# Layer 1 of a two-layer encoder: TensorE's order written out, with own buffers for the gate weights

## The chip, the cores and the metric

The kernel runs on one core of one Trainium2 chip. The metric is the device time of one execution in microseconds (us). TensorE (PE) does the matmuls, ScalarE (ACT) activations, copies and casts, VectorE (DVE) elementwise work and scans, GpSimd (POOL) some elementwise work and small copies; SyncE (SP) only issues the DMAs. Each engine has its own instruction stream; semaphores join them.

## The reference

Two mixing layers over 2048 tokens of width 1024, each closed by a residual and a layer norm. The change concerns layer 1 (the odd layer), cut here to what matters:

```python
u = h @ od_w_in                      # h: modulated x, 2048 x 1024; u: 2048 x 2048
xC, gC = split(u, 2)
xc = causal_conv4(xC, conv_w) + conv_b          # per channel, over time
gate_r = sigmoid(blockdiag(xc, wa) + ba)        # 4 blocks of 256 x 256
gate_i = sigmoid(blockdiag(xc, wx) + bx)
log_a  = -8 * gate_r * softplus(-lam)
a      = exp(log_a)
v      = sqrt(-expm1(2 * log_a)) * (gate_i * xc)
hC     = scan(h_t = a_t * h_(t-1) + v_t)
y      = (hC * silu(gC)) @ od_w_out
x      = layer_norm(alpha * x + (1 + gate) * y)
```

## The kernel before

Channels lie on the 128 partitions, tokens along the free axis. The tokens are worked in two halves of 1024, "blocks of a layer" here, each of two sub-blocks b of 512. The order is layer 0 first half, layer 0 second half, layer 1 first half, layer 1 second half; after each comes an output stage (the product with the output weights in tiles po, the residual r, the layer norm with lg and lb), during which the next half's x is loaded, transposed on TensorE (xp) and scaled to h. Layer 0 is the same before and after.

Every product is done to nearly full fp32 precision by splitting both operands into a rounded part and a residue (names with h and l: hh_h and hl_h for the input, wh_ and wl_ for weights, xh_c and xl_c for the convolved input) and running three matmuls (`mm3`: rounded × residue, rounded × rounded, residue × rounded). A weight piece of 128 × 512 is loaded to a `raw` tile (two buffers for the whole program), cast to wh on ACT, and its residue wl is made on POOL; wh and wl tiles have four buffers each.

In a block of layer 1 `mix1` runs four groups g. A group has two projections (pp_c, channel tiles ct = 2g and 2g+1; 48 matmuls each, 24 for each b). Each 24 are copied from PSUM into u_c on ACT, with a three-token carry (cr_c) on POOL. Then `mix_c` takes the group: it loads the gate weights (raw_wg, wh_wg, wl_wg), convolves u_c into xc_c (one ACT instruction and three on DVE for each channel tile and b), splits xc_c, does the gate matmuls pg_c (two gates × two channel tiles × two inputs × three for each b, 48 for both) with a sigmoid on ACT behind each bank of two PSUM banks, and then over 128 × 2048 elements tanh, exp and square on ACT, two multiplies and an add on DVE, sqrt on ACT (which needs another activation table), the multiply that makes the scan's input (L1191; called gth in the prediction), and two scans on DVE.

After the four groups come eight gate projections (pp_g with silu, `gate_steps`), whose product with the stored scan is the input of the output stage.

The program is written in this order, and a scheduler reorders each engine's instructions by priority; in layer 1 of before TensorE's order is the scheduler's too, while layer 0 writes TensorE's order out by hand. The weight loads run ahead by a priority of 100.

Of the kernel before, what the change touches and what calls it, by code (L numbers as in the profile page):

```python
# [68 lines left out]
def tile_encoder(  # L69
# [19 lines left out]
    nc = tc.nc  # L89
# [10 lines left out]
    wp = ctx.enter_context(tc.tile_pool(name="wp", bufs=4))  # L100
# [16 lines left out]
    tp = _Cur()  # L117
    ps = ctx.enter_context(tc.tile_pool(name="ps", bufs=1, space=PSUM))
# [249 lines left out]
    def split(hi, lo, src, eng=None, hi_eng=None):  # L368
        (hi_eng or nc.scalar.copy)(hi, src)  # L369
        return (eng or nc.vector).tensor_tensor(out=lo, in0=src, in1=hi.bitcast(F32), op=ALU.subtract)  # L370
# [38 lines left out]
                mixer_constants()  # L409
        return hi, lo  # L410

    def load_w(src, name, nk=KT, raws=None, ahead=0):
        with tc.high_priority(offset=ahead):
            return split_w(src, name, nk, raws)

    def split_w(src, name, nk, raws):
        wh, wl = [], []
        for i in range(2):
            n = min(4, nk - 4 * i)
            if raws is None:  # L420
                raw = wp.tile([P, 4, P], F32, name=f"raw_{name}_{i}", tag="raw", bufs=2)[:, 0:n]
                nc.sync.dma_start(raw, src[:, 4 * i : 4 * i + n])
            else:
                raw = raws[:, 4 * i : 4 * i + n]
            hi = wp.tile([P, 4, P], F32R, name=f"wh_{name}_{i}", tag="wh")
            lo = wp.tile([P, 4, P], F32R, name=f"wl_{name}_{i}", tag="wl")
# [24 lines left out]

    def proj(*a, **k):
        for _ in proj_steps(*a, **k):
            pass
# [173 lines left out]
    for i in range(1):  # L628
        t = cst.tile([P, BLK], F32, name=f"st_{i}")
# [170 lines left out]
    for i in range(2):  # L800
        t = cst.tile([P, 8, 64], F32, name=f"tt_{i}")
# [342 lines left out]

    c_state = [None] * 8

    def mix_c(g, sb, us):
        wh, wl = load_w(w_gate[g], f"wg{sb}_{g}", ahead=100)
        nm = f"c{g}_{sb}"
        xc = tp.tile([P, 2, SBT], F32, name=f"xc_{nm}", tag="c_x")  # L1150
        gr = tp.tile([P, 2, SBT], F32, name=f"gr_{nm}", tag="c_gr")
        gi = tp.tile([P, 2, SBT], F32, name=f"gi_{nm}", tag="c_gi")
        for b in range(2):
            ls = slice(b * BLK, (b + 1) * BLK)
            xh = []
            xl = []
            for i in range(2):
                ct = 2 * g + i
                u = us[i][b]
                x_ = xc[:, i, ls]  # L1160
                nc.scalar.activation(
                    x_, u[:, 3 : BLK + 3], AF.Identity, scale=V("conv_w", 24 + ct), bias=V("conv_b", ct)
                )
                for w in range(3):
                    nc.vector.scalar_tensor_tensor(  # L1165
                        out=x_, in0=u[:, w : w + BLK], scalar=V("conv_w", 8 * w + ct), in1=x_,
                        op0=ALU.mult, op1=ALU.add,
                    )
                hi = tp.tile([P, BLK], F32R, name=f"xh{i}_{nm}_{b}", tag=f"c_h{i}", bufs=2)
                lo = tp.tile([P, BLK], F32R, name=f"xl{i}_{nm}_{b}", tag=f"c_l{i}", bufs=2)  # L1170
                split(hi, lo, x_)
                xh.append(hi)
                xl.append(lo)
            for i in range(2):
                ct = 2 * g + i
                for gt, t in enumerate((gr, gi)):
                    pt = ps.tile([P, BLK], F32, name=f"pg_{nm}_{b}_{i}_{gt}", tag="tb", bufs=2)
                    for k in range(2):
                        wi = gt * 4 + k * 2 + i
                        mm3(pt, wh[wi], wl[wi], xh[k], xl[k], k == 0, k == 1)  # L1180
                    nc.scalar.activation(t[:, i, ls], pt, AF.Sigmoid, bias=V(("ba", "bx")[gt], ct))
# [25 lines left out]
    def evac_u(key, ct, nshift, dst):  # L1207
        def evac(b, pt):
            u = up.tile([P, BLK + 3], F32, name=f"u_{key}_{b}", tag="u")
            nc.scalar.copy(u[:, nshift : nshift + BLK], pt)  # L1210
            if nshift:
                prev = carry.get(ct)
                if prev is None:
                    nc.gpsimd.memset(u[:, 0:nshift], 0.0)
                else:
                    nc.gpsimd.tensor_copy(u[:, 0:nshift], prev)
                cr = sp_.tile([P, nshift], F32, name=f"cr_{key}_{b}", tag=f"cr{nshift}_{ct[1]}", bufs=2)
                nc.gpsimd.tensor_copy(cr, u[:, BLK : BLK + nshift])
# [87 lines left out]
        return tail, plan  # L1306

    def mix1(sb, hs, w_first):
        for g in range(4):
            us = [[None, None] for _ in range(2)]  # L1310
            for i in range(2):
                ct = 2 * g + i
                proj(
                    w_od[ct], f"c{sb}_{ct}", hs, evac_u(f"c{sb}_{ct}", (1, ct), 3, us[i]),
                    w_first[0] if ct == 0 else None, ahead=100,
                )
            mix_c(g, sb, us)
        tail = []
        plan = out_weights(1, sb, w_odo, lambda: [
            tp.tile([P, 4, BLK], F32, name=f"wo1_{sb}_{tag}", tag=tag) for tag in ("c_x", "c_gr", "c_gi", "c_th")  # L1320
        ])
        for _ in gate_steps(1, sb, hs, w_od, lambda k: 8 + k, range(KT), tail, plan):
            pass
        return tail, plan

    pre, pre_phase = None, const_phase
# [1 line left out]
    for i, (l, sb) in enumerate(order):  # L1328
        if l:
            w_first = [load_w(w_od[0], f"c{sb}_0")]  # L1330
        elif sb:
            w_first = [load_w(wf_dr[1], f"z{sb}_1")]
        else:
            w_first = [load_w(None, f"z0_{i}", raws=wf[:, i]) for i in (1, 0)]
        hs = make_h(l, sb, pre)
# [4 lines left out]
        with phase(f"mix{l}_{sb}"):  # L1340
            tail, wo = (mix0, mix1)[l](sb, hs, w_first)
# [80 lines left out]
```

## Time and profile before

| | |
|---|---|
| median of 3 runs | 2350.18 us (2343.73 to 2357.08) |
| profiled execution, its own time | 2348.29 us |
| its span in the trace | 2346.6 us |
| busy share | PE 93%, DVE 63%, ACT 54%, POOL 24% |
| mean granted TensorE clock | 0.969 of full speed |
| layer 1, first block | 1672.5 to 1857.1 us, PE busy 169.07 of 184.60 |
| layer 1, second block | 2007.05 to 2194.15 us, PE busy 170.61 of 187.10 |

Times are taken from the start of the span. A row of a timeline gives start, length, engine, line, operation, its output and input tiles (numbers of buffers left out), and in brackets the idle time ahead of it on its engine with what ended it. The numbers behind a stretch are, in this order, its length, the busy time of PE, PEld (weight load), DVE, ACT and POOL, each with its count of instructions, the granted clock, the DMA engines' share and GB/s. A busy matmul reads 0.39 us but the next starts 0.23 us behind it, since they overlap.

### The profile page before, as it was taken

The page shows a single profiled execution, that of the slowest core. Times are in us where ns is not written, and L with a number is a line of the kernel's source. Part 1 is how long each engine was busy: PE and PEld are TensorE (multiplying, and loading weights), DVE is VectorE, ACT ScalarE, POOL GpSimd, SP SyncE. Part 2 cuts the span into 40 slices and gives each one's busy share as a digit, 9 for nine tenths or more (in the row PEclk, how much of TensorE's full clock was granted, in tenths as well). Part 3 has the DMA queues.
Part 4 walks back from the last instruction along what each step waited for, and adds up shares of the span by engine and source line. Part 5 has one row for each costly group of instructions (what it writes and reads, how often), then busy time and mean ns, then how long its engine had stood idle before and what let it go on. Part 6 is the DMA issues. An engine that isn't in the chain of part 4 may idle for free. (4 is left out here: it accounts for less than half of the span.)

```text
span 2346.6 us, 45509 instructions
## 1 busy us (share of the span) xinstructions
PE 2172.6 (93%) x18400; PEld 1727.5 (74%) x18400; DVE 1485.6 (63%) x2750; ACT 1271.8 (54%) x2033; POOL 564.5 (24%) x586
## 2 busy tenths in 40 slices
PE   5989999999999999799999998899999999989998
PEld 4767777777777877577777777678777788767786
DVE  6646676677643678477676666436756556766366
ACT  4344656456666634355665456674467643666541
POOL 3311122212111332112212111112334331353321
PEclk7999999999999999899999999999999999999999
DMA  8310111111332637111111114326312564112652
GB/s 299 95 38 28 35 41 35 43 32 37 110 107 86 221 117 251 35 30 37 35 41 40 40 30 116 112 96 227 133 58 70 173 209 157 63 59 95 206 179 99
DMA packets 185938, 229.82 MB, mean 98 GB/s; under 512 B 65912, under 2 KB 99320, under 8 KB 185728
## 3 DMA queue, kind: packets, MB, share of 16 engines
q1 hardware_dynamic: 185728, 226.92, 30.0%
q8 instruction: 144, 2.36, 0.4%
q14 instruction: 66, 0.54, 0.1%
HBM read 175.46 MB, written 51.39 MB: 97 GB/s over the span
## 5 line engine op out<-in xcount | busy, mean ns | idle before, releaser
L433 PE MATMUL pp_g<-hl_h,wh_g 128*128 128x512 f32 x512 | 210.5, 411 | 4.0 <-ACT go L597 4.0
L435 PE MATMUL pp_g<-hh_h,wl_g 128*128 128x512 f32 x512 | 203.3, 397 | 4.0 <-POOL wl_g L370 4.0
L434 PE MATMUL pp_g<-hh_h,wh_g 128*128 128x512 f32 x512 | 203.0, 397 | 0.0
L370 POOL TENSOR_TENSOR wl_g<-raw_g,wh_g 128x512 fp32r<-128x512 f32 x64 | 97.3, 1525 | 343.9 <-ACT wh_g L369 294.7
L433 PE MATMUL po<-hl_wo,wh_mx 128*128 128x512 f32 x448 | 175.9, 393 | 2.6 <-DVE y L529 2.6
L435 PE MATMUL po<-hh_wo,wl_mx 128*128 128x512 f32 x448 | 175.3, 391 | 0.0
L434 PE MATMUL po<-hh_wo,wh_mx 128*128 128x512 f32 x448 | 174.8, 390 | 0.0
L433 PE MATMUL pp_b<-hl_h,wh_b 128*128 128x512 f32 x384 | 162.6, 423 | 6.2 <-ACT cr_b L851 6.2
L433 PE MATMUL pp_a<-hl_h,wh_a 128*128 128x512 f32 x384 | 165.2, 430 | 0.3 <-ACT cr_b L851 0.3
L435 PE MATMUL pp_a<-hh_h,wl_a 128*128 128x512 f32 x384 | 153.8, 401 | 0.0
L434 PE MATMUL pp_a<-hh_h,wh_a 128*128 128x512 f32 x384 | 153.5, 400 | 0.0
L435 PE MATMUL pp_b<-hh_h,wl_b 128*128 128x512 f32 x384 | 151.8, 395 | 0.0
L434 PE MATMUL pp_b<-hh_h,wh_b 128*128 128x512 f32 x384 | 151.7, 395 | 0.0
L370 POOL TENSOR_TENSOR wl_mx<-raw_mx,wh_mx 128x512 fp32r<-128x512 f32 x64 | 82.2, 1290 | 254.5 <-ACT wh_mx L369 254.5
L370 POOL TENSOR_TENSOR wl_b<-raw_b,wh_b 128x512 fp32r<-128x512 f32 x48 | 69.5, 1451 | 248.6 <-ACT wh_b L369 214.1
L370 POOL TENSOR_TENSOR wl_a<-raw_a,wh_a 128x512 fp32r<-128x512 f32 x48 | 65.9, 1375 | 238.9 <-ACT wh_a L369 238.1
L433 PEld LDWEIGHTS pp_g<-hl_h,wh_g 128*128 128x128 f32 x512 | 98.6, 193 | 27.5 <-ACT go L597 4.8
L435 PEld LDWEIGHTS pp_g<-hh_h,wl_g 128*128 128x128 f32 x512 | 98.1, 192 | 27.3 <-POOL wl_g L370 5.7
L589 DVE TENSOR_TENSOR go<-go,oi 128x512 f32<-128x512 f32 x64 | 46.9, 733 | 110.1 <-DMA oi<-o_dr 65.8
L434 PEld LDWEIGHTS pp_g<-hh_h,wh_g 128*128 128x128 f32 x512 | 98.4, 192 | 18.8
L435 PE MATMUL pp_c<-hh_h,wl_c 128*128 128x512 f32 x256 | 100.8, 395 | 10.9 <-POOL wl_c L370 9.6
L433 PE MATMUL pp_c<-hl_h,wh_c 128*128 128x512 f32 x256 | 101.4, 396 | 2.8 <-DVE hl_h L370 2.6
(368 smaller groups left out, 5731.7 us busy)
## 6 DMA issues: line engine op xcount, KB each, us to landing
adw<-in_ada_w_dram SPq DMA_DIRECT2D x96, 256.0 KB
oi<-o_dr SPq DMA_DIRECT2D x64, 256.0 KB
m_dr<-go SPq DMA_DIRECT2D x56, 256.0 KB
raw_b<-in_w_ev_dram SPq DMA_DIRECT2D x48, 256.0 KB
raw_a<-in_w_ev_dram SPq DMA_DIRECT2D x48, 256.0 KB
raw_g<-in_w_ev_dram SPq DMA_DIRECT2D x32, 256.0 KB
wo<-in_w_evo_dram SPq DMA_DIRECT2D x32, 256.0 KB
raw_mx<-m_dr SPq DMA_DIRECT2D x32, 256.0 KB
```

The costliest lines, as they stand in the source:

```text
L370: return (eng or nc.vector).tensor_tensor(out=lo, in0=src, in1=hi.bitcast(F32), op=ALU.subtract)
L433: nc.tensor.matmul(pt, ah, bl, start=first, stop=False)
L434: nc.tensor.matmul(pt, ah, bh, start=False, stop=False)
L435: nc.tensor.matmul(pt, al, bh, start=False, stop=last)
L589: nc.vector.tensor_mul(go[b], go[b], oi[b])
```

## The change

`mix_c` is split into `c_inputs` (tiles and gate weights) and a generator `c_steps` for each group and b, and `mix1` writes out TensorE's order: a table of steps lets the gate matmuls of a b, in two portions of 12, follow 12 matmuls of a projection each. The first projection of the next group is now under way before a group's first gates, and the last group's gates lie inside the first gate projection. The weights of a projection are loaded one projection ahead. The gate weights' wh and wl get tiles of their own (tags c_wh and c_wl, four buffers each), so that the four of wp are left to the projections; the raw tiles stay shared. The convolved input xc_c has two buffers.

```diff
-    def split_w(src, name, nk, raws):
+    def split_w(src, name, nk, raws, own):
...
-            hi = wp.tile([P, 4, P], F32R, name=f"wh_{name}_{i}", tag="wh")
-            lo = wp.tile([P, 4, P], F32R, name=f"wl_{name}_{i}", tag="wl")
+            hi, lo = (
+                tp.tile([P, 4, P], F32R, name=f"w{c}_{name}_{i}", tag=f"c_w{c}", bufs=4)
+                if own else wp.tile([P, 4, P], F32R, name=f"w{c}_{name}_{i}", tag=f"w{c}")
+                for c in "hl"
+            )
...
+    def c_inputs(g, sb):
+
         nm = f"c{g}_{sb}"
-        xc = tp.tile([P, 2, SBT], F32, name=f"xc_{nm}", tag="c_x")
+        wg = load_w(w_gate[g], f"wg{sb}_{g}", ahead=100, own=True)
+        xc = tp.tile([P, 2, SBT], F32, name=f"xc_{nm}", tag="c_x", bufs=2)
...
+    def c_steps(g, sb, b, us, group):
...
+            xh.append(hi)
+            xl.append(lo)
+            yield (8, 6)[i]
...
+                nc.scalar.activation(t[:, i, ls], pt, AF.Sigmoid, bias=V(("ba", "bx")[gt], ct))
+            if i == 0:
+                yield 2
+        if b == 0:
+            return
         nc.vector.tensor_mul(gi, gi, xc)
...
+            for ct in range(8):
+                g, i = divmod(ct, 2)
+                if i == 0:
+                    groups[g] = c_inputs(g, sb)
+                later = load_w(w_od[ct + 1], f"c{sb}_{ct + 1}", ahead=100) if ct < 7 else None
+                key = f"c{sb}_{ct}"
+                yield from proj_steps(None, key, hs, evac_u(key, (1, ct), 3, us[g][i]), w)
+                w = later
+            yield from gate_steps(1, sb, hs, w_od, lambda k: 8 + k, range(KT), tail, plan)
+
+        tasks = [[16 * g + 4 * b + 4, (g, b)] for g in range(4) for b in range(2)]
...
+        with tc.manual_schedule(engines={nc.tensor.engine}):
```

On TensorE a block read before: projections ct 0 and 1, 12 gate matmuls, 5 of ct 2, the other 36 gate matmuls, and the next gates 103 matmuls on. It now reads: ct 0 to 1, then ct 2 with 12 gate matmuls behind each 12 of its own (12 + 12 + 12 + 12 for the 48 of the group), ct 3 whole (24 + 24), 12 of ct 4, and the next group's first 12 gates. The engines that serve it moved along; two places on ACT and one on SP follow. In the names, wh_c_1_0 is piece 0 of the weights of ct 1, wh_wg_0_1 piece 1 of the gate weights of group 0, u_c_1_0 sub-block 0 of ct 1; of xc_c, xh_c, xl_c, gr_c and gi_c the group's number is left out.

ACT at the start of layer 1's first block, before: the casts of wh_c_1 stand among those of the input ahead of the first copy of a projection.

```order
L369 CAST wh_c_1_0_18051<-raw_c_1_0_18049 128x512
L369 CAST hh_h_0_1_4_17933<-h_0_1_4_17798 128x512
L369 CAST wh_c_1_1_18057<-raw_c_1_1_18055 128x512
...
L1210 COPY u_c_0_0_18014<-pp_c_0_0_17989 128x512
L369 CAST wh_wg_0_0_18123<-raw_wg_0_0_18121 128x512
L1161 ACTIVATE xc_c_0_18133<-u_c_0_0_18014,vec 128x512
L369 CAST wh_wg_0_1_18129<-raw_wg_0_1_18127 128x512
L1210 COPY u_c_0_1_18044<-pp_c_0_1_18019 128x512
```

The same place in the changed kernel.

```order
L1223 COPY u_c_0_0_18043<-pp_c_0_0_18018 128x512
L1223 COPY u_c_0_1_18081<-pp_c_0_1_18056 128x512
L369 CAST wh_wg_0_0_17993<-raw_wg_0_0_17991 128x512
L369 CAST wh_wg_0_1_17999<-raw_wg_0_1_17997 128x512
L1169 ACTIVATE xc_c_0_18003<-u_c_0_0_18043,vec 128x512
L1169 ACTIVATE xc_c_0_18003<-u_c_0_1_18081,vec 128x512
L369 CAST wh_c_1_0_18008<-raw_c_1_0_18006 128x512
L369 CAST wh_c_1_1_18014<-raw_c_1_1_18012 128x512
```

The casts of wh_c_1 moved behind both copies of ct 0, both casts of the gate weights and both first steps of the convolution.

SP at the same time, before: the DMAs that bring the raw pieces, among stores of the residual (x_dr) and loads for the output stage.

```order
L422 DMA raw_c_1_0_18049<-in_w_od_dram 128x512
L422 DMA raw_c_1_1_18055<-in_w_od_dram 128x512
L554 DMA x_dr<-r_1_6_17716 128x1024
L422 DMA raw_wg_0_0_18121<-in_w_gate_dram 128x512
L422 DMA raw_wg_0_1_18127<-in_w_gate_dram 128x512
L554 DMA x_dr<-r_1_7_17812 128x1024
L422 DMA raw_c_2_0_18252<-in_w_od_dram 128x512
L513 DMA r_0_0_19786<-x_dr 128x1024
```

And in the changed kernel.

```order
L422 DMA raw_wg_0_0_17991<-in_w_gate_dram 128x512
L422 DMA raw_wg_0_1_17997<-in_w_gate_dram 128x512
L557 DMA x_dr<-r_1_6_17716 128x1024
L557 DMA x_dr<-r_1_7_17812 128x1024
L422 DMA raw_c_1_0_18006<-in_w_od_dram 128x512
L422 DMA raw_c_1_1_18012<-in_w_od_dram 128x512
L422 DMA raw_c_2_0_18094<-in_w_od_dram 128x512
```

The gate weights moved ahead of ct 1. The loads r_0_0, r_0_1, lg_0 and lb_0 for the output stage, which stood here, moved to right ahead of x_1_0_0, the first load of x for the next half, in the output stage itself.

ACT behind the last gate matmul of group 0, before: from the last sigmoid to the sqrt.

```order
L1181 ACTIVATE gi_c_0_18135<-pg_c_0_1_1_1_18224,vec 128x512
L1186 ACTIVATE th_c_0_18235<-gr_c_0_18134 128x2048
L1187 ACT_TABLE_LOAD
L1187 ACTIVATE gr_c_0_18134<-gr_c_0_18134 128x2048
L1210 COPY u_c_2_0_18289<-pp_c_2_0_18264 128x512
L1188 ACTIVATE xc_c_0_18133<-gr_c_0_18134 128x2048
L369 CAST wh_wg_1_0_18398<-raw_wg_1_0_18396 128x512
L369 CAST wh_wg_1_1_18404<-raw_wg_1_1_18402 128x512
L1210 COPY u_c_2_1_18319<-pp_c_2_1_18294 128x512
L1190 ACT_TABLE_LOAD
L1190 ACTIVATE th_c_0_18235<-th_c_0_18235 128x2048
```

And in the changed kernel, a row further, to the next group's xh_c.

```order
L1190 ACTIVATE gi_c_0_18005<-pg_c_0_1_1_1_18333,vec 128x512
L369 CAST wh_wg_2_1_18465<-raw_wg_2_1_18463 128x512
L1199 ACTIVATE th_c_0_18344<-gr_c_0_18004 128x2048
...
L369 CAST xh_c_0_1_18365<-xc_c_0_18194 128x512
L1201 ACTIVATE xc_c_0_18003<-gr_c_0_18004 128x2048
L369 CAST wh_c_5_0_18474<-raw_c_5_0_18472 128x512
L1223 COPY u_c_3_0_18406<-pp_c_3_0_18381 128x512
L1169 ACTIVATE xc_c_0_18194<-u_c_3_0_18406,vec 128x512
L369 CAST wh_c_5_1_18480<-raw_c_5_1_18478 128x512
L1203 ACT_TABLE_LOAD
L1203 ACTIVATE th_c_0_18344<-th_c_0_18344 128x2048
L369 CAST xh_c_0_0_18415<-xc_c_0_18194 128x512
```

A cast of gate weights moved between sigmoid and tanh; two casts of ct 5, an xh_c and an xc_c of the next group moved into the chain; the second xh_c of the next group's sub-block 0 stands behind the sqrt.

## Rows read from the trace of the kernel before

**Rows 1.** The page's first part: busy us, share of the span, instructions.

```profile
PE 2172.6 (93%) x18400; PEld 1727.5 (74%) x18400; DVE 1485.6 (63%) x2750; ACT 1271.8 (54%) x2033; POOL 564.5 (24%) x586
```

**Rows 2.** The table of stretches: layer 1's first block, an output stage, its second block.

```profile
1672.50:1857.10 184.60, 169.07 (x724) 133.86 (x722) 120.75 (x118) 124.93 (x156) 72.58 (x67) 1.00 0.28 92
...
1911.40:2006.00 94.60, 93.89 (x441) 77.80 (x440) 65.47 (x100) 40.98 (x64) 25.27 (x21) 1.00 0.46 160
2007.05:2194.15 187.10, 170.61 (x723) 134.88 (x721) 121.20 (x118) 124.73 (x156) 75.48 (x67) 0.99 0.23 77
```

**Rows 3.** TensorE's waits, 1672.5 to 2194.15: us in total, times, longest.

```profile
PE pg_c L433 <- DVE xl_c L370: 9.8, 8, 1.6
PE pp_c L435 <- POOL wl_c L370: 9.6, 5, 3.1
PE pp_g L435 <- POOL wl_g L370: 4.0, 4, 1.3
PE pp_c L433 <- DVE hl_h L370: 2.6, 2, 1.3
PE pp_g L433 <- ACT go L597: 2.0, 1, 2.0
PE pp_c L435 <- POOL u_c L1214: 1.3, 1, 1.3
...
PE pg_c L433 <- ACT gr_c L1181: 0.6, 1, 0.6
```

**Rows 4.** TensorE's timeline around its longest wait in layer 1.

```profile
2107.81 0.39 PE L434 MATMUL pp_c<-hh_h,wh_c 128*128 128x512 f32 x1
2111.28 0.50 PE L435 MATMUL pp_c<-hh_h,wl_c 128*128 128x512 f32 x1 [3.08 <-POOL wl_c L370]
...
2115.27 0.40 PE L433 MATMUL pp_c<-hl_h,wh_c 128*128 128x512 f32 x1
2115.50 0.39 PE L434 MATMUL pp_c<-hh_h,wh_c 128*128 128x512 f32 x1
```

**Rows 5.** The table of stretches behind that wait.

```profile
2112.00:2114.00 2.00, 2.00 (x6) 1.58 (x5) 2.00 (x4) 0.00 (x0) 0.48 (x1) 0.50 0.81 266
```

**Rows 6.** ACT's timeline, at a block's start and at a raw piece's landing.

```profile
1671.03 0.62 ACT L369 CAST wh_c<-raw_c 128x512 fp32r<-128x512 f32 x1 [0.50 <-PE po L434]
...
1686.77 0.58 ACT L1210 COPY u_c<-pp_c 128x512 f32<-128x512 f32 x1
...
1756.34 0.62 ACT L369 CAST wh_wg<-raw_wg 128x512 fp32r<-128x512 f32 x1 [0.63 <-DMA raw_wg<-in_w_gate_dram]
```

**Rows 7.** DVE's timeline, at the block's start and at the first group's end.

```profile
1684.69 0.69 DVE L370 TENSOR_TENSOR hl_h<-h,hh_h 128x512 fp32r<-128x512 f32 x1
...
1724.68 2.29 DVE L1191 TENSOR_TENSOR gi_c<-gi_c,th_c 128x2048 f32<-128x2048 f32 x1 [3.20 <-ACT th_c L1190]
```

**Rows 8.** POOL's timeline: two residues of weights.

```profile
1686.95 1.44 POOL L370 TENSOR_TENSOR wl_wg<-raw_wg,wh_wg 128x512 fp32r<-128x512 f32 x1 [0.23 <-ACT wh_wg L369]
...
2102.25 2.86 POOL L370 TENSOR_TENSOR wl_c<-raw_c,wh_c 128x512 fp32r<-128x512 f32 x1 [2.74 <-ACT wh_c L369]
```

**Rows 9.** SP's issues: a raw piece, and six loads of x.

```profile
1753.23 0.33 SPq L422 DMA_DIRECT2D raw_wg<-in_w_gate_dram  x1
...
1920.81 2.73 SPq L388 DMA_DIRECT2D x<-x_dr  x6
```

**Rows 10.** TensorE's timeline: behind group 0's gates, and the first transposes.

```profile
1710.52 0.40 PE L435 MATMUL pp_c<-hh_h,wl_c 128*128 128x512 f32 x1
...
1928.98 0.82 PE L391 MATMUL xp<-ident,x 128*128 128x128 f32 x6
```

**Rows 11.** ACT's timeline inside the first group's end.

```profile
1713.65 1.28 ACT L1187 ACT_TABLE_LOAD   x1
1714.95 1.92 ACT L1187 ACTIVATE gr_c<-gr_c 128x2048 f32<-128x2048 f32 x1
```

**Rows 12.** The table of stretches while x is loaded, in the first output stage.

```profile
1925.00:1930.00 5.00, 5.00 (x28) 4.23 (x27) 2.57 (x5) 1.43 (x3) 2.30 (x2) 1.00 0.99 384
```

More of the change, by code (lines that the diff above doesn't have):

```diff
@@ L410, in make_h, with load_w @@
         return hi, lo
-    def load_w(src, name, nk=KT, raws=None, ahead=0):
+    def load_w(src, name, nk=KT, raws=None, ahead=0, own=False):
         with tc.high_priority(offset=ahead):
-            return split_w(src, name, nk, raws)
-    def split_w(src, name, nk, raws):
+            return split_w(src, name, nk, raws, own)
+    def split_w(src, name, nk, raws, own):
         wh, wl = [], []
@@ L1145, in tile_encoder @@
     c_state = [None] * 8
-    def mix_c(g, sb, us):
-        wh, wl = load_w(w_gate[g], f"wg{sb}_{g}", ahead=100)
+    def c_inputs(g, sb):
         nm = f"c{g}_{sb}"
-        xc = tp.tile([P, 2, SBT], F32, name=f"xc_{nm}", tag="c_x")
+        wg = load_w(w_gate[g], f"wg{sb}_{g}", ahead=100, own=True)
+        xc = tp.tile([P, 2, SBT], F32, name=f"xc_{nm}", tag="c_x", bufs=2)
         gr = tp.tile([P, 2, SBT], F32, name=f"gr_{nm}", tag="c_gr")
         gi = tp.tile([P, 2, SBT], F32, name=f"gi_{nm}", tag="c_gi")
[L1153 to L1162, printed above, removed]
-                )
[L1164 to L1181, printed above, removed]
@@ new lines, in c_inputs @@
+        return wg, xc, gr, gi
+    def c_steps(g, sb, b, us, group):
+        (wh, wl), xc, gr, gi = group
+        nm = f"c{g}_{sb}"
+        ls = slice(b * BLK, (b + 1) * BLK)
+        xh, xl = [], []
+        for i in range(2):
+            ct = 2 * g + i
+            u = us[i][b]
+            x_ = xc[:, i, ls]
+            nc.scalar.activation(
+                x_, u[:, 3 : BLK + 3], AF.Identity, scale=V("conv_w", 24 + ct), bias=V("conv_b", ct)
+            )
+            for w in range(3):
+                nc.vector.scalar_tensor_tensor(
+                    out=x_, in0=u[:, w : w + BLK], scalar=V("conv_w", 8 * w + ct), in1=x_,
+                    op0=ALU.mult, op1=ALU.add,
+                )
+            hi = tp.tile([P, BLK], F32R, name=f"xh{i}_{nm}_{b}", tag=f"c_h{i}", bufs=2)
+            lo = tp.tile([P, BLK], F32R, name=f"xl{i}_{nm}_{b}", tag=f"c_l{i}", bufs=2)
+            split(hi, lo, x_)
+            xh.append(hi)
+            xl.append(lo)
+            yield (8, 6)[i]
+        for i in range(2):
+            ct = 2 * g + i
+            for gt, t in enumerate((gr, gi)):
+                pt = ps.tile([P, BLK], F32, name=f"pg_{nm}_{b}_{i}_{gt}", tag="tb", bufs=2)
+                for k in range(2):
+                    wi = gt * 4 + k * 2 + i
+                    mm3(pt, wh[wi], wl[wi], xh[k], xl[k], k == 0, k == 1)
+                nc.scalar.activation(t[:, i, ls], pt, AF.Sigmoid, bias=V(("ba", "bx")[gt], ct))
[3 more added lines that the diff above has]
+            return
@@ L1308, in mix1 @@
     def mix1(sb, hs, w_first):
[L1309 to L1317, printed above, removed]
         tail = []
         plan = out_weights(1, sb, w_odo, lambda: [
-            tp.tile([P, 4, BLK], F32, name=f"wo1_{sb}_{tag}", tag=tag) for tag in ("c_x", "c_gr", "c_gi", "c_th")
-        ])
@@ L1322, in mix1, with projections @@
-        for _ in gate_steps(1, sb, hs, w_od, lambda k: 8 + k, range(KT), tail, plan):
-            pass
+            tp.tile([P, 4, BLK], F32, name=f"wo1_{sb}_{tag}", tag=tag, bufs=bufs)
+            for tag, bufs in (("c_x", 2), ("c_gr", 1), ("c_gi", 1), ("c_th", 1))
+        ])
+        us = [[[None, None] for _ in range(2)] for _ in range(4)]
+        groups = {}
+        def projections():
+            w = w_first[0]
+            for ct in range(8):
[7 more added lines that the diff above has]
+            yield from gate_steps(1, sb, hs, w_od, lambda k: 8 + k, range(KT), tail, plan)
@@ new lines, in mix1 @@
+        tasks = [[16 * g + 4 * b + 4, (g, b)] for g in range(4) for b in range(2)]
+        steps = projections()
+        now = 0
+        with tc.manual_schedule(engines={nc.tensor.engine}):
+            while tasks or steps is not None:
+                if steps is not None and next(steps, "end") == "end":
+                    steps = None
+                now += 1
+                for entry in list(tasks):
+                    if entry[0] > now:
+                        continue
+                    if isinstance(entry[1], tuple):
+                        g, b = entry[1]
+                        entry[1] = c_steps(g, sb, b, us[g], groups[g])
+                    wait = next(entry[1], None)
+                    if wait is None:
+                        tasks.remove(entry)
+                    else:
+                        entry[0] = now + wait
```

## The prediction

> **What bounds the kernel now.** I read the engines' shares first: TensorE is busy 93% of the span, no other engine above 63% [rows 1]. So the time is TensorE's matmuls plus its holes. The table of stretches shows where the holes are [rows 2]: each of the two blocks of layer 1 that the change rewrites lasts about 186 us and has some 16 us in which TensorE does nothing, while the output stage between them has under 1. The matmul count stays, so the change is worth what it does to those holes.
>
> The list of TensorE's waits over both blocks splits them [rows 3]: xl_c 9.8 us, wl_c 9.6, wl_g 4.0, the memset of u_c 1.3, gr_c 0.6: 25.3 us in 19 waits. The waits for hl_h (2.6) and for go (2.0) come from work that the change does not touch, so I leave them. A wait costs a little more than its row: around the longest, start to start is 3.47 us (2107.81 to 2111.28) where the row says 3.08 and a matmul's pace is 0.23, so 0.16 comes on top [rows 4].
>
> The clock is full (1.00) in the first block and 0.99 in the second [rows 2]. That hundredth lies behind this wait: after 3.08 us of nothing the granted clock fell to 0.50, the lower level of 1.2 GHz [rows 5], and the ten matmuls to 2115.27 took 3.99 us instead of 2.30 [rows 4], of which 1.6 is the clock's.
>
> **What the change removes.** At best all 19 waits: 25.3 + 19 × 0.16 = 28.3 us, and the 1.6 of the clock: 29.9 us. I credit it all, wl_g included, although nothing in the change speeds up wl_g. The least that it can remove is nothing, which would make it slower still.
>
> **What it adds: the start of a block.** Before, wh_c of the second projection was cast while the stage before still ran (the last cast at 1671.03 [rows 6]). Now the raw pieces of the first gate weights go ahead of it. There are two raw buffers, so raw_c_1_0 can only be sent for once wl_wg_0_0 has been made, and on ACT the casts of wh_wg stand behind both copies of the first projection. By rows: the last hl_h is done at 1684.69 + 0.69 = 1685.4 [rows 7], its three matmuls end at 1686.1; copy u_c 0.58, cast of wh_wg 0.62 [rows 6] to 1687.5 (with the small gaps between); wl_wg 1.44 [rows 8] to 1689.0; a raw piece reached its cast 3.1 us after its issue (1753.23 to 1756.34 [rows 6, 9]), so 1692.1; cast 0.62, wl_c 1.44: 1694.3. TensorE wants it with the third matmul, at 1686.6: **7.7 us**. With wl at 2.86 [rows 8], twice, it is 10.5; below 7 only if the load is faster than the one shown.
>
> Each later raw pair follows 5.2 us (3.1 + 0.62 + 1.44) behind the one ahead. So raw_c_3_0 leaves at about 1704.9, lands at 1708.0, and its cast stands on ACT ahead of the last xh of the first gates: xl_c is done at about 1710.0 where TensorE, after 60 matmuls and three of the gates, wants it at 1708.1: 1.9. The next cast, copy, xc_c, xh_c and a table load stand ahead of the first sigmoids: a bank that TensorE wants at 1715.1 comes at 1717.5: 2.4. The start costs 7.7 + 1.9 + 2.4 = 12.0; if the raw chain catches up, 7.7.
>
> **What it adds: a group's end.** Behind the last gate matmul of a group ACT and DVE do sigmoid, tanh, table load, exp, square, table load, sqrt and two multiplies. In before this ended at 1724.68 + 2.29 = 1726.97 [rows 7], 16.45 us after the gates had left TensorE at 1710.52 [rows 10], and cost nothing, since 103 matmuls (23 us) stand between two groups' gates. Now 24 + 24 + 12 stand there, 13.65 us, and TensorE wants the second xl_c of the next group 0.7 later, at 14.35. On DVE that xl_c now stands behind gth, on ACT its xh_c behind the sqrt. With before's own tail it comes at 16.45 + 0.7 = 17.15: 2.8 late.
>
> The tail also gets longer. Counted from the gates' end: gi sigmoid to 0.8; then the cast of the last wh_wg, whose raw piece waits for a wl_c, which waits for a weight tile that TensorE reads until −2.8: −2.8 + 0.6 + 1.6 + 3.1 = 2.5, cast to 3.1; tanh to 5.0, table load and exp (1.28 and 1.92 [rows 11]) to 8.0, xh_c, square to 10.4, a cast, a copy to 11.6, xc_c, a cast, table load to 14.3, sqrt to 16.2, gth to 18.5, xl_c to 19.2: **4.9** late (0.8 of it in a wait for the copy's bank, 4.1 in one for xl_c). This holds for two of the three boundaries in a block; at the third no gate weights are loaded, and the 2.6 in which ACT waits for them falls out: 2.3. Together 12.1; with before's tail 2.8 + 2.8 + 0.2 = 5.8.
>
> The last group's gates lie behind the first gate projection, whose silu table alternates with theirs: two more loads of 1.28 ahead of the sigmoids, of which the second bank hides about 1.2: 1.4, at least 0. Each wait of 4.1 is longer than the one of 3.08 that dropped the clock, so 2 × 1.6 = 3.2; at least 0. The drop after the start's wait is taken up by the two waits behind it.
>
> **What it adds: the output stage of the first block.** r_0_0, r_0_1, lg and lb, four times 0.5 MB, were sent for early in the block; now they stand on SP's queue right ahead of the x loads. At the 384 GB/s seen there [rows 12] 2 MB are 5.5 us. The x loads were issued at 1920.81 [rows 9] and the first transpose ran at 1928.98 without a wait [rows 10]. What had landed by about 1927.3 now comes at 1932.8: 3.8; nothing, if r is sent for earlier. In the second block they had this place before.
>
> **Moved at no price.** The gate weights' own tiles and the second xc_c add no instruction. Three more table loads a block lie on ACT, busy 125 of 185 us [rows 2]; uncovered they cost 1.28 each, which the chains above hold.
>
> **Sum.** A block: 12.0 + 12.1 + 1.4 + 3.2 = 28.7; two 57.4; output stage 3.8: 61.2. Less 29.9: +31.3. The profiled execution took 2348.3, of which the span is 2346.6; that gives 2379.6. It lies 1.9 under the median of 2350.2, so 2380 to 2381: **2380**.
>
> Low end: 7.7 + 5.8 a block, no clock, no x: 27.0 − 29.9 gives 2345. High end: the start with wl at 2.86 (+2.8) and what follows it late by as much again (+2.8), 11.2 on two blocks, 2391; the clock drop at the start and at the third boundary too, 4 × 1.6, 2397.
>
> **A rule against the trace.** Behind a table load the next ACTIVATE starts at once: 1713.65 + 1.28 = 1714.93, exp at 1714.95 [rows 11]. The Trainium skill, "ScalarE: Activation LUTs", section "What ACT_TABLE_LOAD costs", gives about 1283 ns for the load, as here, and about 1380 ns of drain besides. This trace does not show the drain in that place, and the row decides.
>
> **Rivals.** (a) *ACT never waits for a raw piece* (faster): then a group's end is down to its own links, 0.7 + 1.92 + 1.28 + 1.92 + 1.92 + 2.29 + 1.92 + 2.29 + 0.7 = 14.9 [rows 7, 11], and only 0.55 late. With the start at 7.7 that is 6 × 0.55 + 15.4 − 29.9, 2337; with the start's pieces there too, 2322. It decides from boundaries of about 0.5 us down. For it: a pair of loads needs 5.2 us where a projection gives 10.9. Against: the other casts, copies and xc_c that the order puts into the tail, in turn.
>
> (b) *New holes equal the old ones*: start 7.7 alone and boundaries by before's own tail, 2345; with half of the x term and one clock drop in each block, 2350. For it: the raw chain has 5 us of slack in each projection to catch up with.
>
> (c) *A table switch costs more than its 1.28*: as much again at two switches in each of six boundaries, 12 × 1.28 = 15: 2395. Against it the row above. By the rule's 1380 ns (the Trainium skill, same page and section) it would be 16.6 and 2396; the trace disagrees.
>
> (d) *Lateness carries on*: a group that ends late sends for its weights late, and the next boundary pays again; 4 us more at each of four later boundaries give 2396, and 2403 and over if the gate projections inherit it.
>
> **How the numbers follow.** The forecast as summed, with its own range 2360 to 2402: 0.65. (a) 0.08. (b) 0.18. (c) 0.03, (d) past 2402 0.06. A measurement of this kernel tells about 0.5% from no change, 2338.4 to 2361.9. (a) is faster; (b) and the bottom edge of the forecast the same; the rest slower: 0.08, 0.20, 0.72. The range takes in the low end and (b), and leaves out (a) and the far part of (d): 2342 to 2402.
>
> **What would show it.** In the changed kernel's list of TensorE's waits: one of 7 to 8 us for wl_c or wh_c at the start of each block, with ACT's cast of wh_c idle ahead of it for the load of raw_c; xl_c waits of some 4 us at two boundaries a block instead of 1.2 on average; a granted clock under 1.00 behind those; a wait for x at the first transposes of the first output stage. What would make it wrong: blocks under 187 us, raw pieces landing before ACT reaches their casts, or gth done within 60 matmuls of the gates.

## The result and the profile after

The changed kernel takes 2373.72 us (median of 4 runs, 2370.72 to 2378.68) against 2347.93 for the kernel before: a ratio of 1.0101, with an interval of 1.0075 to 1.0127. It is slower by 1%; the forecast was 2380. The profiled execution took 2373.62, its span is 2371.9, 25.3 more than before.

The first part of the page, and the table of stretches (layer 1's first block up to its output stage, that stage, the second block):

```profile
PE 2185.5 (92%) x18400; PEld 1739.5 (73%) x18400; DVE 1485.7 (63%) x2750; ACT 1278.9 (54%) x2039; POOL 556.9 (23%) x586
```

```profile
1672.34:1922.36 250.02, 230.12 (x962) 184.72 (x961) 142.74 (x139) 154.43 (x204) 91.52 (x81) 0.96 0.33 109
1922.36:2023.57 101.21, 98.15 (x451) 80.89 (x449) 64.47 (x101) 37.34 (x57) 21.39 (x18) 0.97 0.49 173
2023.57:2274.15 250.58, 230.33 (x962) 184.77 (x961) 142.98 (x140) 153.84 (x203) 91.81 (x80) 0.96 0.33 109
```

The same stretches of the kernel before. They start and end with the first and last matmul of a block, while those of [rows 2] stop at 1857.1 and 2194.15, inside the gate projections:

```profile
1672.50:1911.41 238.91, 223.38 (x963) 178.82 (x961) 141.02 (x138) 146.55 (x194) 89.63 (x78) 1.00 0.38 124
1911.41:2007.05 95.64, 94.93 (x450) 78.72 (x449) 66.52 (x101) 41.32 (x65) 26.23 (x22) 1.00 0.46 158
2007.05:2248.48 241.43, 224.94 (x962) 179.86 (x961) 142.91 (x140) 147.44 (x196) 92.64 (x78) 0.99 0.34 112
```

The 25 us are 11.1 in the first block, 9.2 in the second and 5.6 in the output stage between; the last stage is 0.4 shorter. The same matmuls take 6.7 and 5.4 us more of TensorE's busy time in the blocks: that is the clock, now 0.96. TensorE's idle time in a block grew by less, from 15.5 to 19.9 us and from 16.5 to 20.3. The list of TensorE's waits from 1672.3 to 2200 answers to [rows 3]:

```profile
PE pg_c L436 <- DVE xl_c L370: 23.3, 6, 4.7
PE pp_c L436 <- ACT wh_c L369: 11.7, 2, 5.9
PE pg_c L436 <- ACT gr_c L1190: 2.9, 4, 0.9
PE xp L391 <- DMA x<-x_dr: 2.6, 3, 0.9
PE pp_c L436 <- DVE hl_h L370: 1.1, 2, 0.6
PE pp_c L438 <- POOL wl_c L370: 0.8, 2, 0.4
PE xp L391 <- PE po L438: 0.5, 1, 0.5
...
```

All waits of before on wl_g, the memset of u_c and go are gone and those for wl_c nearly so; six for xl_c and two for wh_c, all long, stand in their place. At a block's start TensorE waits for the weights of the second projection; ACT casts them as soon as they have landed, behind the gate weights:

```profile
1690.52 0.79 PE L436 MATMUL pp_c<-hl_h,wh_c 128*128 128x512 f32 x1 [5.89 <-ACT wh_c L369]
```

```profile
1685.15 1.14 ACT L369 CAST wh_wg<-raw_wg 128x512 fp32r<-128x512 f32 x2
...
1689.85 0.62 ACT L369 CAST wh_c<-raw_c 128x512 fp32r<-128x512 f32 x1 [2.15 <-DMA raw_c<-in_w_od_dram]
```

TensorE's timeline at the first group's end shows both parts of the price, the wait and the slow matmuls behind it:

```profile
1741.91 0.40 PE L438 MATMUL pg_c<-xh_c,wl_wg 128*128 128x512 f32 x1
1747.03 0.51 PE L436 MATMUL pg_c<-xl_c,wh_wg 128*128 128x512 f32 x1 [4.71 <-DVE xl_c L370]
...
1748.18 0.63 PE L436 MATMUL pg_c<-xl_c,wh_wg 128*128 128x512 f32 x1
1748.61 0.63 PE L437 MATMUL pg_c<-xh_c,wh_wg 128*128 128x512 f32 x1
```

Three matmuls of the gates run, the fourth waits 4.71 us (5.12 start to start), and the next ones come every 0.43 us instead of 0.23. Why xl_c is late, on ACT and on DVE:

```profile
1729.55 0.62 ACT L369 CAST wh_wg<-raw_wg 128x512 fp32r<-128x512 f32 x1 [1.36 <-DMA raw_wg<-in_w_gate_dram]
1730.08 1.92 ACT L1199 ACTIVATE th_c<-gr_c 128x2048 f32<-128x2048 f32 x1
...
1738.56 0.82 ACT L1169 ACTIVATE xc_c<-u_c,vec 128x512 f32<-128x512 f32 x1
...
1739.91 1.28 ACT L1203 ACT_TABLE_LOAD   x1
1741.20 1.91 ACT L1203 ACTIVATE th_c<-th_c 128x2048 f32<-128x2048 f32 x1
1744.20 0.62 ACT L369 CAST xh_c<-xc_c 128x512 fp32r<-128x512 f32 x1 [1.09 <-DVE xc_c L1173]
```

```profile
1739.78 4.38 DVE L1173 SCALAR_TENSOR_TENSOR xc_c<-u_c,vec,xc_c 128x512 f32<-128x512 f32 x3
1744.09 2.28 DVE L1204 TENSOR_TENSOR gi_c<-gi_c,th_c 128x2048 f32<-128x2048 f32 x1
1746.29 0.68 DVE L370 TENSOR_TENSOR xl_c<-xc_c,xh_c 128x512 fp32r<-128x512 f32 x1
1746.89 4.46 DVE L1209 TENSOR_TENSOR_SCAN hc_c<-gr_c,gi_c 128x1024 f32<-128x1024 f32 x2
```

ACT holds the tanh back for a raw piece, the sqrt ends at 1743.11, DVE starts gth at 1744.09 behind three convolutions, and xl_c comes behind gth. These three convolutions are those of the awaited xl_c itself: their first step stands on ACT at 1738.56, behind the square, and the cast of its xh_c waits for them until 1744.20. With xh_c done at 1744.82, the place behind gth costs xl_c some 1.4 us; the rest of its lateness is that its own convolution comes late.

### The profile page after: what moved, and what is told of

It is laid out like the page before. It is cut to its first block, busy times and chain, and to the rows that moved or that the text cites. A ratio compares the mean times of both kernels' runs of the same rounds, so it can differ in the third digit from the quotient of the medians.

```text
span 2371.9 us, 45518 instructions
## 1 busy us (share of the span) xinstructions
PE 2185.5 (92%) x18400; PEld 1739.5 (73%) x18400; DVE 1485.7 (63%) x2750; ACT 1278.9 (54%) x2039; POOL 556.9 (23%) x586
## 3 DMA queue, kind: packets, MB, share of 16 engines
q1 hardware_dynamic: 185728, 226.92, 29.9%
q8 instruction: 144, 2.36, 0.4%
## 5 line engine op out<-in xcount | busy, mean ns | idle before, releaser
L370 POOL TENSOR_TENSOR wl_g<-raw_g,wh_g 128x512 fp32r<-128x512 f32 x64 | 91.4, 1429 | 363.7 <-ACT wh_g L369 313.9
L1173 DVE SCALAR_TENSOR_TENSOR xc_c<-u_c,vec,xc_c 128x512 f32<-128x512 f32 x96 | 97.7, 1026 | 61.2 <-ACT xc_c L1169 24.3
```

Of the source, the lines that this page charges most:

```text
L1173: nc.vector.scalar_tensor_tensor(out=x_, in0=u[:, w : w + BLK], scalar=V("conv_w", 8 * w + ct), in1=x_, op0=ALU.mult, op1=ALU.add,)
```

## The experiments

Each was timed against the kernel before on the same chip. A block's length, below, is from its first projection matmul to the first po in the profiled execution; the first block begins between 1668.4 and 1679.5 us, depending on the run, so lengths are compared, not places.

| kernel | ratio (interval) | first block | output stage | second block |
|---|---|---|---|---|
| before | 1 | 239.1 | 95.4 | 241.7 |
| changed | 1.0101 (1.0075 to 1.0127) | 250.3 | 101.0 | 250.8 |
| second xc_c alone (e6) | 1.0068 (1.0050 to 1.0085) | 247.8 | 100.3 | 244.7 |
| own tiles alone (e5) | 1.0067 (1.0045 to 1.0089) | 245.2 | 103.2 | 246.8 |
| both buffers, old order (e4) | 1.0108 (1.0079 to 1.0136) | 252.6 | 102.5 | 250.9 |
| order alone (e9) | 1.0306 (1.0272 to 1.0340) | 278.1 | 94.4 | 277.9 |
| order, own tiles (e7) | 1.0356 (1.0323 to 1.0390) | 280.3 | 101.6 | 280.7 |
| changed, ct 1 first (e1) | 1.0043 (1.0022 to 1.0064) | 244.7 | 99.7 | 245.0 |
| changed, gates in one run (e2) | 1.0107 (1.0064 to 1.0149) | 249.9 | 98.1 | 250.3 |
| e1 and e2 (e3) | 1.0141 (1.0109 to 1.0173) | 256.9 | 101.6 | 253.7 |
| changed, tiles apart (e10) | 1.0165 (1.0141 to 1.0188) | 258.7 | 103.7 | 257.7 |
| e1, convolution first (e11) | 1.0152 (1.0129 to 1.0174) | 254.1 | 100.5 | 254.5 |
| e11, two gr_c and gi_c, x first (e12) | 0.9913 (0.9892 to 0.9934) | 230.8 | 94.4 | 231.1 |
| e12 without the priority (e13) | 0.9998 (0.9979 to 1.0016) | 241.9 | 94.4 | 241.0 |

### The start, and the gates' distance (e1, e2, e3)

e1 exchanges two lines:

```diff
+                later = load_w(w_od[ct + 1], f"c{sb}_{ct + 1}", ahead=100) if ct < 7 else None
                 if i == 0:
                     groups[g] = c_inputs(g, sb)
-                later = load_w(w_od[ct + 1], f"c{sb}_{ct + 1}", ahead=100) if ct < 7 else None
```

> The changed kernel, with the load of the second projection's weights written ahead of the first gate weights of each group (two lines exchanged). My theory: the wait of 6.1 + 0.7 us for wh_c and wl_c at the start of each block comes from that order alone; it goes, with the 2.3 to 2.5 us of slow matmuls behind it: 2 x 9.2 = 18 less than the changed kernel's 2372 of span, 2354. The waits at the groups' ends stay at 4.9, 4.9 and 2.4. Rival: with two raw buffers the chain of loads is too slow in any order, and the wait only moves to the next weights (ct 2 or the first gates): less than 6 us gained, 2366 or more.

The wait for wh_c at a block's start and the slow matmuls behind it are gone, as expected (9.1 us in the first block). But a block is only 5.6 and 5.8 us shorter. In the first block smaller waits grew or came new, start to start: hl_h 1.72 instead of 0.70, xl_c in the first group 1.51, gr_c 1.33, 1.03 and 2.61 instead of 0.53, none and 1.01: 6.0 us given back, while the first two groups' ends fell from 4.89 to 3.42. So the loads' order takes part in the start's wait; the expectation that nothing else would move fell. What still separates e1's blocks from those of before is hardly idle time: TensorE is idle for 16.3 and 16.6 us in them (15.5 and 16.5 before). Its matmuls take 5.0 and 3.5 us longer, at a granted clock of 0.97, since the idle time lies in fewer and longer waits.

e2 puts 96 matmuls instead of 60 between two groups' gates:

```diff
-            yield (8, 6)[i]
+            yield (8, 6 if b else 10)[i]
...
-            if i == 0:
-                yield 2
```

> The changed kernel, with a group's 48 gate matmuls in one run behind 12 matmuls of the second sub-block of the next projection, so that 96 matmuls (21.8 us) stand between two groups' gates instead of 60 (13.7 us). My theory: the waits at a group's end are the tail's 18.6 us less the cover; all six go (24.3 us) with the slow matmuls behind them (11) and about 1 of each block's last group: 36 less, 2336; the start's waits stay. Rival: ACT and not the cover is what is short there; the gate banks wait for their sigmoids in the run instead, 3 us and more per group, eight times: 24 given back, 2360.

Nothing is gained. The scheduler moved DVE's order along with the later gates. In e2, at the first group's end on DVE:

```profile
1743.41 2.28 DVE L1202 TENSOR_TENSOR gi_c<-gi_c,th_c 128x2048 f32<-128x2048 f32 x1
1745.61 0.68 DVE L370 TENSOR_TENSOR xl_c<-xc_c,xh_c 128x512 fp32r<-128x512 f32 x1
1746.21 4.46 DVE L1207 TENSOR_TENSOR_SCAN hc_c<-gr_c,gi_c 128x1024 f32<-128x1024 f32 x2
1750.60 0.66 DVE L370 TENSOR_TENSOR xl_c<-xc_c,xh_c 128x512 fp32r<-128x512 f32 x1
```

The xl_c that TensorE wants now stands behind the two scans as well, so it is 3.1 us late again, and the last group's gates wait 4.6 for a bank. Cover alone does not help while the scheduler places the wanted instruction behind other work.

> Both edits of the two runs above together. My theory: they are independent, 18 + 36 less: 2318, faster than the kernel before (2347) by 1.2%. Rival: with the start early, ACT and POOL run into the first gates' casts, so that one edit hides part of the other: 2330 or more.

Both together are worse than either. The gates' banks wait: 36.3 us for gr_c, up to 6.3 each. On ACT the casts of the gate weights, now sent for last, hold up the first sigmoids:

```profile
1743.53 0.62 ACT L369 CAST wh_wg<-raw_wg 128x512 fp32r<-128x512 f32 x1 [5.86 <-DMA raw_wg<-in_w_gate_dram]
1747.24 0.62 ACT L369 CAST wh_wg<-raw_wg 128x512 fp32r<-128x512 f32 x1 [3.09 <-DMA raw_wg<-in_w_gate_dram]
...
1752.67 0.69 ACT L1190 ACTIVATE gr_c<-pg_c,vec 128x512 f32<-128x512 f32 x1
```

### The parts one by one (e4, e5, e6, e7, e9)

e4 is the kernel before with own tiles and the second xc_c; e5 has the tiles alone, e6 xc_c alone; e7 is the changed kernel with one xc_c, e9 with neither buffer.

```diff
+            hi, lo = (tp.tile(..., tag=f"c_w{c}", bufs=4) if own else wp.tile(...) for c in "hl")
...
-        xc = tp.tile([P, 2, SBT], F32, name=f"xc_{nm}", tag="c_x")
+        xc = tp.tile([P, 2, SBT], F32, name=f"xc_{nm}", tag="c_x", bufs=2)
```

> The kernel before, in its own order, with only the gate weights' own tiles and the second xc_c. My theory: the tiles bring none of the new waits on weights and at groups' ends, and take away those on wl_c (some 8 of 9.6 us); but they fill the memory in which the output stage's r lay, so that r, lg and lb are sent for right ahead of x here too, and the first transposes wait as in the changed kernel (5.6 us more for the output stage): 2342 to 2348. Rival: the order has nothing to do with r and x, and the tiles alone are a gain of 8 to 12 us: 2335 to 2338; or the tiles themselves bring the wait of 6 us at a block's start: 2356 and more.

The buffers alone, in the old order, cost as much as the whole change. The waits on wl_c are gone as expected and x is late as expected, but waits for xl_c are there, 33.2 us in 10. In e4, on DVE behind group 0:

```profile
1725.48 6.27 DVE L1168 SCALAR_TENSOR_TENSOR xc_c<-u_c,vec,xc_c 128x512 f32<-128x512 f32 x6
1731.66 2.29 DVE L1194 TENSOR_TENSOR gi_c<-gi_c,th_c 128x2048 f32<-128x2048 f32 x1
```

Six convolutions of the next group stand between the two multiplies of this one, which one xc_c had not allowed: it was in use until the first. The expectations of the next two runs tell that theory and its rival apart.

> The kernel before with only the gate weights' own tiles (one xc_c). Theory after the run with both buffers: what made that one slow is the second xc_c, which lets convolutions of the next group run between a group's sqrt chain (six of them, 6.3 us, on DVE ahead of gth); the tiles by themselves take away some 8 us of wl_c waits and cost the 7 us of r before x: no wait for xl_c above 2.5 us, 2340 to 2350. Rival: the tiles did it, by moving casts of weights into the chain: xl_c waits of 4 us and more here, 2362 and up.

> The kernel before with only the second xc_c (gate weights in the shared tiles). By the theory the waits for xl_c of 4 to 6 us at groups' ends are here, with DVE's convolutions ahead of gth, and r before x: 2362 to 2378. By the rival the kernel is as before but for r and x: 2350 to 2355.

Both were half right. With xc_c alone the xl_c waits of 5 us are there (two), in all 15.0 us, and on DVE six convolutions stand ahead of gth as in e4; other waits grew beside them (8.3 us for wl_g, 4.0 before), for which no cause was sought. With the tiles alone waits for xl_c are there too, 31.1 us in 8, up to 5.3, but not for that reason: on DVE the first block's order is that of before but for the place of one xl_c at the first gates. The first group's end in e5, and in before:

```profile
1739.55 0.80 PE L436 MATMUL pg_c<-xl_c,wh_wg 128*128 128x512 f32 x1 [3.96 <-DVE xl_c L370]
```

```profile
1733.83 0.50 PE L435 MATMUL pp_c<-hh_h,wl_c 128*128 128x512 f32 x1 [2.05 <-POOL wl_c L370]
...
1738.02 0.50 PE L433 MATMUL pg_c<-xl_c,wh_wg 128*128 128x512 f32 x1 [1.62 <-DVE xl_c L370]
```

The wait for wl_c is gone, and TensorE waits 3.96 us for xl_c instead of 2.05 and 1.62, since xl_c comes no earlier (40.2 us behind the first gates' xl_c, 39.3 before). Only at the first gates did casts move into the chain, as the rival says: those of wh_c, waiting for their loads, stand ahead of xh_c, and the wait there is 3.74 us instead of 1.19. Over its blocks TensorE is idle for 17.1 and 17.4 us (15.5 and 16.5 before), in 6 waits each instead of 12 and 11, and the matmuls behind these longer waits are slow:

```profile
1669.99:1915.21 245.22, 228.15 (x963) 184.84 (x962) 142.18 (x139) 146.42 (x194) 91.29 (x78) 0.96 0.34 111
```

So neither buffer alone is to blame, and they do not harm in the same way. That x is late comes with either of them: each moves r behind (output stage 100.3 and 103.2), and where neither is there it does not happen. That it is the memory they take, which r needs, is argued, not shown.

> The changed kernel with one xc_c. If the second one is pure harm, the waits at the groups' ends shrink from 4.9 to under 3 and the time falls to 2358 or less. My expectation: with the gates only 60 matmuls apart one tile is worse, since the next group's convolutions then wait for the square and the multiply of this group: 7 us and more at each of the six boundaries, 2380 to 2400.

> The changed kernel without either buffer: the written order alone, one xc_c and shared weight tiles. In the first block's output stage r is sent for early again: no wait at the first transposes of x there, 6 to 7 us less. The groups' ends as in the changed kernel with one xc_c (my expectation: 7 us and more each), the start's wait of 6 us is there in any case, since the gate weights stand ahead of the second projection's: 2375 to 2395. Rival: the order is a gain and the buffers ate it: under 2350.

With the written order, one xc_c costs 30 us a block (e7; 27 to 28 in e9, which has the shared weight tiles too): 80.1 (e7) and 78.6 us (e9) of waits for xl_c, 12 each, up to 9.6 us, more than expected. The order therefore needs the second xc_c (1.0356 without it, 1.0101 with it), while in the old order the same buffer alone costs 16 us. In e9 r is sent for early in the first block and its output stage takes 94.4 us: so late x costs the changed kernel 101.0 − 94.4 = 6.6 us. And in e9 the wait at a block's start is absent, although the gate weights go ahead of the second projection as in the changed kernel: that spoke against the prediction's reason for it.

### Why a block starts late (e10)

```diff
-                tp.tile([P, 4, P], F32R, name=f"w{c}_{name}_{i}", tag=f"c_w{c}", bufs=4)
+                wp.tile([P, 4, P], F32R, name=f"w{c}_{name}_{i}", tag=f"c_w{c}", bufs=2)
```

> The changed kernel with the gate weights' own tiles in the pool of the other weight tiles (two buffers each) instead of in the memory of the block, which the output stage before still holds; the order of the loads is unchanged, gate weights ahead of the second projection. If the wait of 6 us at a block's start comes from where the tiles lie (their first cast must wait until the last r of the stage before is stored), it is gone, with the slow matmuls behind it: 2352 to 2358, and the waits at the groups' ends stay at 4.9, 4.9, 2.4. If it comes from the order of the loads and of ACT's casts alone, as in the prediction, the wait stays: 2368 and more.

The wait at the start is gone with the loads in the same order. ACT casts the first gate weights in the stage before, at 1664.98, where the changed kernel did so at 1685.15:

```profile
1664.98 0.62 ACT L369 CAST wh_wg<-raw_wg 128x512 fp32r<-128x512 f32 x1 [0.56 <-DMA raw_wg<-in_w_gate_dram]
```

So the start's wait takes both: gate weights sent for first (e1 takes that away) and their tiles in the block's memory (e9 and e10 take that away). In the changed kernel the raw piece had been sent for at 1659.02 and its cast came 26 us later. That the stage before holds this memory until then is the likely reason; no run looks at it by itself. With two buffers instead of four, though, waits for wh_c of 5.4 us came at the groups' ends (six, 32.3 us), and the kernel is slower as a whole.

### What a group's end needs (e11, e12, e13)

e11 is e1 with a priority for three things:

```diff
+            with tc.high_priority() if nshift else nullcontext():
+                nc.scalar.copy(u[:, nshift : nshift + BLK], pt)
...
+            with tc.high_priority():
                 (the convolution of xc_c and its split)
```

> The kernel with the second projection's weights first (e1_c1_first), and with a priority for the copy of a projection, the convolution and the split of xc_c, so that on ACT and DVE the next group's xl_c stands ahead of the sqrt and of gth, and casts of gate weights behind them. My theory of a group's end (TensorE waits for xl_c because it stands behind gth): the six waits for xl_c of 2.4 to 3.4 us go. The scans end no earlier, and the next sigmoids wait for gr_c and gi_c, so some 1 to 3 us for a bank come instead: 2340 to 2350. Rival: the tail as a whole is what is too long for 60 matmuls, and the same time comes back as waits for gr_c: 2357 and more.

The rival's case, and more so. The six waits for xl_c are gone, and six waits of 5.9 to 8.0 us for gr_c stand in their place. On ACT, e11's first sigmoid of group 1:

```profile
1745.42 1.28 ACT L1191 ACT_TABLE_LOAD   x1
1751.19 0.69 ACT L1191 ACTIVATE gr_c<-pg_c,vec 128x512 f32<-128x512 f32 x1 [4.49 <-DVE hc_c L1210]
```

It waits 4.49 us for the scans, which still read the only gr_c and gi_c. The changed kernel had this second limit too, hidden behind the first; there ACT's next sigmoids stand behind this:

```profile
1751.43 1.28 ACT L1190 ACT_TABLE_LOAD   x1 [5.28 <-DVE hc_c L1209]
```

e12 gives those two a second buffer and sends for x ahead of r:

```diff
-        gr = tp.tile([P, 2, SBT], F32, name=f"gr_{nm}", tag="c_gr")
-        gi = tp.tile([P, 2, SBT], F32, name=f"gi_{nm}", tag="c_gi")
+        gr = tp.tile([P, 2, SBT], F32, name=f"gr_{nm}", tag="c_gr", bufs=2)
+        gi = tp.tile([P, 2, SBT], F32, name=f"gi_{nm}", tag="c_gi", bufs=2)
...
+                    with tc.high_priority():
+                        nc.sync.dma_start(xt[j], x1_dr[t0 + j * P : t0 + (j + 1) * P, :])
```

> As e11_conv_first, with two buffers for gr_c and gi_c (the next sigmoids no longer wait for the scans) and with x sent for ahead of r, lg and lb. By my theory then no wait above 1.5 us is left in a block of layer 1 and none for x: each block falls to about 226 us (from 239 and 241 in the kernel before, 250 in the changed one): 2320 to 2330, faster than the kernel before. Rival: ACT, with three more table loads a block, or DVE, cannot keep this pace, and the wait only moves to the banks of the gates: 2340 and more.

2331.07 us, 0.9913 of the kernel before: the version that beats both. Its waits in the first block, and its stretches:

```profile
PE pg_c L437 <- ACT gr_c L1192: 5.2, 4, 1.7
PE pp_c L437 <- DVE hl_h L370: 1.5, 1, 1.5
PE pp_g L437 <- ACT go L601: 0.9, 1, 0.9
PE pg_c L437 <- DVE xl_c L370: 0.8, 1, 0.8
```

```profile
1677.07:1907.89 230.82, 222.31 (x963) 179.41 (x962) 144.03 (x141) 152.15 (x202) 89.03 (x80) 1.00 0.36 119
1907.89:2002.26 94.37, 94.37 (x450) 78.63 (x448) 65.92 (x99) 38.27 (x59) 26.02 (x20) 1.00 0.53 184
```

No wait is longer than 1.8 us, the clock is full, x is not waited for. The expectation of 2320 to 2330 was a little low: gr_c keeps up to 1.8 at a group's gates.

> As e12_two_gates without the priority for copy, convolution and split: the second projection's weights first, two buffers for gr_c and gi_c, x ahead of r. On DVE xl_c of the next group stands behind gth again. If both links of a group's end count, the waits for xl_c come back as in e1_c1_first (3.4, 3.4, 2.4 us in each block, with slow matmuls behind them of 1.5 to 2.8), and the time is e12's 2331 plus 2 x 13 less the gr_c waits of 1.8 that they hide: 2345 to 2356. If the second gr_c and gi_c alone made the gain, it stays at 2328 to 2336.

Without the priority the waits for xl_c are back (3.43, 3.43 and 2.37 us in the first block), a block takes 241.9 and the time is that of the kernel before. Both links count: the priority, which brings the copy, the convolution and xl_c ahead of the sqrt and gth, and the second gr_c and gi_c. Which of the priority's three parts matters most was not tested.

## Why the prediction came out

**What is removed.** Sized at 29.9, it was more. The new holes of the two blocks (28.3 and 28.9, below) and of the output stage (5.6) make 62.8, where the span grew by 25.3: 37.5 were removed. I had left out the waits for go and hl_h as untouched. The two for go (2.17 and 2.14 us start to start) are gone, and the two for hl_h fell from 1.48 to 0.70 and 0.75: 5.8 of the missing 7.6.

**The start.** Forecast 12.0, of which 7.7 for the second projection's weights: 6.06 + 0.72 in the first block, 5.93 + 0.84 in the second, with the load's 2.7 us (issue 1687.14, cast 1689.85) where I took 3.1. The two waits behind it came to 0.53 us in the first block and 0.96 in the second, instead of 4.3. What stood there instead was the clock (2.3 and 2.5 us of slow matmuls), which I had counted at nothing because those waits would take it up. It went the other way round.

**The reason for the start** was half of it. I named the order of the loads and of ACT's casts; e10 shows that where the tiles lie decides that order, since the same loads in the same order do not make TensorE wait when the tiles are free early.

**A group's end.** Forecast 4.9, 4.9 and 2.3; measured 4.89, 4.89 and 2.36 in both blocks. The gates left TensorE at 1727.29. The raw piece that holds up the tanh came 2.3 us behind that (forecast 2.5), the sqrt ended 15.8 behind it (16.2), all as argued. The last link was another than I wrote: I had xl_c wait for gth alone and put nothing for its own convolution, but that ended at 1744.17, after the sqrt, and gth began behind it, 1.0 us after the sqrt's end. So xl_c was done 19.7 behind the gates instead of 19.2, and TensorE, which starts that group at 14.2 rather than 13.65, wanted it as much later. The total agrees partly by this accident. What I did not see is the next limit, the scans that hold gr_c and gi_c (e11).

**The clock** at the groups' ends was sized at 3.2 a block and was 5.6 and 5.5: 1.6, 2.4 and 1.6. The third, behind 2.20 us of nothing, I had counted as free, since I knew only of the wait of 3.08 that had dropped the clock [rows 4, 5]. **The last group**, forecast 1.4, was 1.01 and 1.07.

**The block's sum**, forecast 28.7: 6.78 + 0.53 + 2.3 + 12.14 + 5.6 + 1.0 = 28.3 and 6.77 + 0.96 + 2.5 + 12.13 + 5.5 + 1.1 = 28.9. That the sum fits is luck in part: the start's waits were 4.7 us (second block 4.3) under the forecast, and the clock cost 4.7 us (4.8) over the 3.2 that I had put for it.

**The output stage**, forecast 3.8: 5.6, and 6.6 beside the one in e9 without that wait, most of the difference to the forecast being clock again (2.1 us of slow matmuls behind the transposes). The 1927.3 from which I counted x's lateness is an estimate of mine that no row shows.

**The rivals.** That every table switch costs more is refuted once more: the load of 1739.91 ends at 1741.19 and the sqrt starts at 1741.20. So the drain that the Trainium skill names ("ScalarE: Activation LUTs", section "What ACT_TABLE_LOAD costs") is not in this trace at that place either. That lateness carries on did not happen: the second boundary is as late as the first. That the order works at all (rival a) is true only with more than the change brings; e12 shows what. In the changed kernel ACT did wait for a raw piece, 1.36 us ahead of the cast at 1729.55. Rival b needed boundaries by the tail of before, 2.8 us late; the first two were 4.89.

## What to carry to other kernels

When one engine's order is written by hand and the others stay with a scheduler, read for each wait of that engine what stands ahead of the releasing instruction on the others: three edits here (e2, e3, e11) moved the wait, and only the one that cleared both links (e12) beat the kernel before. A buffer more is not free: it can give a scheduler room to put work ahead of what is wanted (e4, e6), and something that was loaded early (r here) can lose its place. Look at how idle time is cut up, and not only at its sum: e1 and e5 had hardly more of it than the kernel before, in fewer and longer waits, and lost 3.5 to 5 us a block to the clock. And where a tile lies can decide when it is filled, whatever its load's priority says (e10).

## What the runs showed of the hardware

Elementwise work on DVE and POOL can hold each other up. Three convolutions of 128x512 on DVE took 4.38 us at 1739.78 in the changed kernel; in e12 three took 2.33 while POOL did nothing:

```profile
1734.39 2.33 DVE L1175 SCALAR_TENSOR_TENSOR xc_c<-u_c,vec,xc_c 128x512 f32<-128x512 f32 x3
```

In the changed kernel POOL made residues of weights at the same time. The first and the third convolution, beside one residue each, took 1.78 us; the second, beside copies of three tokens only, took 0.75:

```profile
1742.38 1.78 DVE L1173 SCALAR_TENSOR_TENSOR xc_c<-u_c,vec,xc_c 128x512 f32<-128x512 f32 x1
```

```profile
1738.12 2.89 POOL L370 TENSOR_TENSOR wl_c<-raw_c,wh_c 128x512 fp32r<-128x512 f32 x1 [5.06 <-ACT wh_c L369]
...
1742.36 1.26 POOL L370 TENSOR_TENSOR wl_c<-raw_c,wh_c 128x512 fp32r<-128x512 f32 x1
```

The one that began first was not held up: the residue of 2.89 us began inside a multiply of DVE (1737.57 to 1739.86), which took 2.29 us, no longer than elsewhere, while the residue of 1.26 us began just ahead of the third convolution. The Trainium skill says so ("SBUF — State Buffer", section "Who interferes with whom"): a DVE instruction with two inputs in SBUF and a GpSimd one that reads SBUF take turns at a pair of ports. The rows fit that; no run here tested it alone.

The granted clock fell behind shorter waits than I knew of from [rows 4]: behind 2.20 us at 1824.56 the matmuls from 1826.2 on came every 0.43 us (0.50 granted from 1826.5 to 1828.5, the level of 1.2 GHz), while 2.05 us in the kernel before left the pace alone. Each of the six waits of 4.7 us and more in the layer 1 blocks of the changed kernel had slow matmuls behind it, 1.6 to 2.5 us worth: such a wait cost a third to a half more than its row.

```profile
1826.50:1828.50 2.00, 2.00 (x6) 1.51 (x6) 2.00 (x2) 0.00 (x0) 0.64 (x1) 0.50 0.43 131
```
